# A hybrid decoder layer: products without use on TensorE in the gaps of the first transposes and of the router, and another order of the token blocks

## The chip, the cores and the metric

The kernel runs on one core of one Trainium2 chip. A core has TensorE (PE; its weight loads are listed as PEld), VectorE (DVE), ScalarE (ACT), GpSimd (POOL) and SyncE (SP), which here mostly starts transfers, and 16 DMA engines. [...] The metric is the device time of one execution, in microseconds, as the median of several runs.

## What is computed

A decoder layer for 512 tokens of width 1024 with 16 learned tokens in front: a normed input goes through one large projection into two mixers, attention and a state-space scan, whose outputs are gated, merged and added to the input; then each token goes through the best two of eight experts of its best group of four. Cut to what matters here:

```python
h = jnp.concatenate([meta, x], axis=1)               # 16 + 512 tokens
u = rmsnorm(h, norm_mix)
proj = u @ w_in                                      # 1024 -> cq, ckv, kr, z, xbc, dt, g_attn, g_ssm
merged = (sigmoid(g_attn) * (mla_branch(...) @ w_branch_attn)
          + sigmoid(g_ssm) * (ssd_branch(...) @ w_branch_ssm))
h = h + merged @ w_out
v = rmsnorm(h, norm_ffn)
g_idx = argmax(v @ w_group + b_group)                # coarse: one of 4 groups
top_vals, top_idx = top_k((v @ w_expert + b_expert)[group g_idx], 2)   # fine: 2 of 8
out = sum over experts e of comb[:, e] * ((silu(v @ w_gate[e]) * (v @ w_up[e])) @ w_down[e])
result = rmsnorm(h + out, norm_final)[:, 16:]
```

## The kernel before

The layer is written as one function with the Tile framework. Most of its instructions are put in order by a scheduler that works with its own estimate of times; where order matters, a block `with in_order(...)` fixes the order of the named engines to that of the code.

**Start.** The 528 tokens lie in five blocks: 0 to 3 of 128 and block 4 of 16. For each, `u_rstd` (L182) makes the root mean square, with ScalarE's squares `junk` and GpSimd's power. `u_turn` (L203) multiplies by that and by the gain vector `gmix` and turns the block on TensorE, four 128x128 transposes into a PSUM tile `pt` per half. Where `u_gain` (L195) has already multiplied the gain on GpSimd, ScalarE does the rest of the scaling, else VectorE does both in one instruction. `u_split` (L215) copies the turned half twice, as a rounded part `uh` on ScalarE and the rest `ul` on VectorE. Weights are split in the same way (`win0h`, `win0l`). A product of the projection is then three products, high by high, high by low and low by high. `first_mm(j, i)` (L318) makes that for weight tile j and the half i of the tokens: `first0a` and `first1a` for the first 256 tokens, `first0b` and `first1b` for the other 272. The block from L324 sets the order of all five engines' queues there.

**Middle.** Projection, scan, attention, merging and the output product keep TensorE busy from there to about 560 us.

**Router.** Around the output product's last pieces (`pout`), the rows of `h` are turned (`pvT`), multiplied with the router's weights (`plg`), and per block of tokens VectorE finds the group and the two experts (`choose`). `rank` (L1285) counts with products `rk` how many earlier tokens chose the same expert, `find_slots` and `place` (L1316) put each token's number and weight at its place in tiles `tb` and `tw` through small products, and VectorE makes of `tb` the list `idx`. Here TensorE, VectorE, ScalarE and GpSimd run in the order of the code.

**Experts.** Tokens of two experts at a time are gathered from DRAM by GpSimd (`gather`, into `xg`), 16 pairs in all. For each pair TensorE turns them (`pxT`), multiplies with the gate and up weights (`gu`, 2 MB for each expert, in two halves) and the down weights (`dn`, 1 MB), and adds the results up per token (`pc`). Seven places for `gu` and seven for `dn` are filled by transfers that SyncE starts in the order of its queue; a place is filled again when TensorE has read it. Expert 4's `gu` is loaded behind a small write, `fence` (L1429), of 128 values of four bytes each, that waits for a flag which GpSimd sets behind the first three gathers. A branch (L1446) around a part for overfull experts, that isn't taken here, stands between the router and the experts in every engine's queue.

Of the kernel before, what the change touches and what calls it, by code (L numbers as in the profile page):

```python
# [11 lines left out]
BF16 = mybir.dt.bfloat16  # L12
# [61 lines left out]
def hybrid_layer(ctx: ExitStack, tc, A, out):  # L74
# [34 lines left out]
    def ps(name):  # L109
        return psp.tile([128, 512], F32, tag="ps", name=name)  # L110
# [4 lines left out]
    def btile(name, dt=F32, n=L, tag="u"):  # L115
        t = big.tile([128, KD * L], dt, tag=tag, name=name, bufs=2 if tag == "u" else 1)
        return t[:, :KD * n].rearrange("p (k n) -> p k n", k=KD)
# [24 lines left out]
    one1 = cp.tile([1, 4], F32, name="one1")  # L142
    dve.memset(one1, 1.0)
    act.activation(one1[0:1, 0:1], one1[0:1, 0:1], AF.Square)
    xin = btile("xin", n=T, tag="v").rearrange("p k n -> p (k n)").rearrange("p (b n) -> p b n", b=4)
    xt = [[xin[:, i, hh * 512:(hh + 1) * 512] for hh in range(2)] for i in range(4)] + [glist("xm", 2, n=T, p=gq)]
    gmix = glist("gmix", 2, n=T, p=gq)
# [15 lines left out]
    load_x(1)  # L163
    load_x(2)
    ic = cs("ic")
    trib, onesb = cp.tile([128, 128], BF16, name="trib"), cp.tile([128, 128], BF16, name="onesb")
    identb, maskb = cp.tile([128, 128], BF16, name="identb"), cp.tile([128, 128], BF16, name="maskb")

    def rstd_small(dst, ssum, n, p=128, w=1):
# [25 lines left out]
    def u_gain(i, hh):  # L195
        p = 128 if i < 4 else NM
        xx = xt[i][hh][:p]
        pool.tensor_tensor(xx, xx, gmix[hh][:p], op=ALU.mult)
        gained.add((i, hh))
# [46 lines left out]
    chunk, wins = [None], {}  # L246
# [66 lines left out]
        return r  # L313


    first = [[ps(f"first{j}{x}")[:, :n] for x, n in zip("ab", (256, 272))] for j in range(2)]

    def first_mm(j, i):  # L318
        (wh, wl), (n0, n1) = wins[j], HALF[i]
# [2 lines left out]
                pe.matmul(first[j][i], x[:, k], y[:, k, n0:n1], start=(n == 0 and k == 0), stop=(n == 2 and k == KD - 1))  # L322

    with in_order(act, dve, pool, pe, nc.sync):  # L324
        u_rstd(0)
        u_turn(0, 0)
        u_rstd(1)
        u_turn(0, 1)
        u_gain(1, 1)
        u_turn(1, 0)  # L330
        u_rstd(2)
        u_gain(2, 0)
        u_gain(2, 1)
        u_turn(1, 1)
        u_split(0, 0)
        u_split(0, 1)
        u_split(1, 0)
        u_split(1, 1)
        wins[0] = proj_w(0)
        load_x(4)  # L340
        load_x(3)
        first_mm(0, 0)
        u_rstd(4)
        u_rstd(3)
        u_gain(3, 0)
        u_gain(3, 1)
        u_turn(2, 0)
        u_turn(2, 1)
        wins[1] = proj_w(1)
        first_mm(1, 0)  # L350
        nc.sync.dma_start(pv, A["pv"])
        nc.sync.dma_start(cst[:, 128:], A["cst"][:, 128:])
        nc.sync.dma_start(alog, bcast_row(A["alog"], H))

        u_turn(4, 0)
        u_turn(4, 1)
        u_split(2, 0)
        u_split(2, 1)
        u_turn(3, 0)
        u_turn(3, 1)  # L360
        u_split(4, 0)
        u_split(4, 1)
        u_split(3, 0)
        u_split(3, 1)
    for j in range(2):
        first_mm(j, 1)
    for d_, s_ in ((trib, cs("before")), (onesb, ones), (identb, ident), (maskb, mask_s)):
# [976 lines left out]
    with in_order(pe):  # L1344
        turn(0, 0)
        turn(1, 0)
        po0 = out_half(0, lambda: logits(0, 0), lambda: logits(1, 0), lambda: turn(2, 0))
        po1 = out_half(1, lambda: (logits(2, 0), turn(0, 1, po0)), lambda: turn(3, 0), lambda: (logits(0, 1), norm_v(0)))
        glx.close()
        mws["d"] = ctx.enter_context(tc.tile_pool(name="mwd", bufs=1, reuse_waits="tile", side="right"))  # L1350
        load_gu(5)
        for i in range(3, ND):
            if DN_AT[i] == "d":
                load_dn(i)
        po2 = out_half(2, lambda: (logits(3, 0), turn(1, 1, po1)), lambda: None, lambda: (logits(1, 1), norm_v(1)))
        c0, c2, c3 = choose(0, 2), choose(2, 3), choose(3, 4)
        steps(c0, 4)
        po3 = out_half(3, lambda: turn(2, 1, po2), lambda: (norm_v(2), steps(c0)), lambda: (logits(2, 1), rank(0)))
        in_turn = ctx.enter_context(ExitStack())
        in_turn.enter_context(in_order(act, dve, pool))  # L1360
        steps(c2, 5)
        find_slots(0)
        copies = turn(3, 1, po3)
        steps(c2, 3)
        copies()
        norm_v(3)
        weigh_exp(0)
        steps(c2)
        logits(3, 1)
        rank(2)  # L1370
        weigh(0)
        place(0, tb, 2)
        weigh_exp(2)
        steps(c3, 10)
        steps(c3)
        find_slots(2)
        rank(3)
        place(2, tb, 2)
        cnt = ps("cnt")
        for b in range(4):  # L1380
            pe.matmul(cnt[:, :32], onesb, oh12s[b][:, :32], start=(b == 0), stop=(b == 3))
        place(0, tw, 3)
        find_slots(3)
        weigh_exp(3)
        place(3, tb, 2)
        ovf, ovi = sm.tile([128, 1], F32, tag="sq1", name="ovf", bufs=4), cp.tile([128, 1], I32, name="ovi")
        dve.tensor_reduce(ovf, cnt[:, :32], axis=AX.X, op=ALU.max)
        dve.tensor_scalar(ovi, ovf, CAP + 0.5, None, op0=ALU.is_gt)
        weigh(2)
        lpos = cp.tile([128, 16], F32, name="lpos")  # L1390
        wsl, rsl = cp.tile([128, 16], F32, name="wsl"), cp.tile([128, 16], F32, name="rsl")
        idx = cp.tile([128, 16], I32, name="idx")
        dve.tensor_scalar(idx, tb[:, :16], float(NONE), None, op0=ALU.add)
        weigh(3)
        place(2, tw, 3)
        place(3, tw, 3)
        act.activation(lpos, tw[:, 16:32], AF.Copy)
        act.activation(wsl, tw[:, :16], AF.Copy, scale=2.0)
        in_turn.close()
# [234 lines left out]
                                 op0=ALU.mult, op1=ALU.mult)  # L1634
        dve.tensor_mul(gtab[:, :, 1], goh, ic[:, 105:109, None].to_broadcast([128, 4, 4]))

    pg = ps("pg")[:, :16].rearrange("p (b v g) -> p b v g", b=2, v=2)

    def group_places():
        for h in range(2):  # L1640
# [47 lines left out]
    LC = [slice(0, 512), slice(512, 1024)]  # L1688

    with in_order(act, dve, pe, pool, nc.sync):  # L1690
        for hh in range(2):
            turn_x(0, hh)
        group_tables()
        for p in range(16):
            end = p and p % 4 == 0
            expert_gu(p)
            for h in range(2):
                for e in (2 * p, 2 * p + 1):
                    if e != EV:
                        load_gu(e + NR + (e < EV), (h,))  # L1700
            if p < 15:
                turn_x(p + 1, 0)
                turn_x(p + 1, 1)
                if p:
                    combine(p - 1, 0, (0,))
                expert_h(p)
                if p == 0:
                    group_places()
                else:
                    combine(p - 1, 0, (1,))  # L1710
                    combine(p - 1, 1)
                y_start(p)
                y_rest(p)
                for hh in range(2):
                    for f in range(2):
                        y_mm(p, f, hh)
                    y_split(p, hh)
                    if end:
                        for b in range(2):
                            squares(b, hh)  # L1720
            else:
                y_start(p)
                y_rest(p)
                combine(p - 1, 0)
                expert_h(p, (0,))
                combine(p - 1, 1, (0,))
                y_mm(p, 0, 0)
                expert_h(p, (1,))
                y_mm(p, 0, 1)
                y_mm(p, 1, 0)  # L1730
                y_split(p, 0)
                y_mm(p, 1, 1)
                y_split(p, 1)
                combine(p - 1, 1, (1,))
            for e in range(max(2 * p + 6, ND), min(2 * p + 8, 30)):
                load_dn(e)
            if p == 12:
                for c in LC:
                    load_dn(30, [c])
                    load_dn(31, [c])  # L1740
            if p == 0:
                group_lists()
            if p == 2:
                load_gain()
            if end:
                for b in range(2):
                    norm(b)
                for b in range(2):
                    for hh in range(2):
                        scale(b, hh)  # L1750
                    store(p // 4 - 1, b)
        junk = ev.tile([128, KD, 128], F32, tag="xT", name="junk", bufs=1).rearrange("p k n -> p (k n)")
        for b in range(2):
            combine(15, 0, (b,))
            squares(b, 0, junk[:, :512])
            gained(b, 0)
        for b in range(2):
            combine(15, 1, (b,))
        squares(0, 1, junk[:, :512])
        squares(1, 1, junk[:, 512:])  # L1760
        norm(0)
        norm(1)
        for b in range(2):
            scale_gained(b, 0)
            scale(b, 1)
            store(3, b)
# [117 lines left out]
```

## Time and profile before

| | us |
|---|---|
| median of 3 runs | 820.62 |
| lowest and highest | 819.89, 820.73 |
| the profiled execution | 818.55 |
| its span, first to last instruction | 816.8 |
| TensorE busy in the span | 773.5 (95%) |
| VectorE, ScalarE, GpSimd busy | 453.8, 299.6, 141.3 |

The profile is of one execution. Times in it are counted from its first instruction. Matmuls are pipelined and their ends are modelled, so neighbours overlap a little. One product of float32 operands shows as two records of a pass each, so a row can count twice as many products as the program has. A wait in brackets at a row's end is the idle time of that engine just before it, with what ended it.

### The profile page before, as it was taken

What the parts mean: (1) busy time and instruction counts of PE and PEld (TensorE: products, weight loads), DVE (VectorE), ACT (ScalarE), POOL (GpSimd) and SP (SyncE); (2) the same over time, 40 slices, a digit from 0 to 9 for tenths busy, and PEclk for the clock granted to TensorE, in tenths of its full rate; (3) what the DMA queues carried; (4) which work ended last, traced back from release to release, by engine and by line L of the source; (5) the groups of instructions that cost most, each with busy time, mean ns of one, the idle gap of its engine ahead of it and who ended that gap; (6) DMA issues with size and microseconds to landing.
All of it is one profiled execution on the core that took longest, in us unless ns stands there. A gap on an engine that the chain in (4) does not pass through costs nothing.

```text
span 816.8 us, 11335 instructions
## 1 busy us (share of the span) xinstructions
PE 773.5 (95%) x4202; PEld 530.7 (65%) x4202; DVE 453.8 (56%) x1013; ACT 299.6 (37%) x566; POOL 141.3 (17%) x197
## 2 busy tenths in 40 slices
PE   4999999999999999999999899997799999999995
PEld 3999987677778878876665678886334343434342
DVE  3697528975366445486776766516334444543523
ACT  6554425333224473164654232422112322322313
POOL 5100002334111100005353400004100110200201
PEclk9999999999999999999999999997799999999998
DMA  7312216343222215020212395587899999999990
GB/s 256 110 58 101 104 60 203 100 129 117 91 73 95 103 41 187 29 62 9 66 41 79 92 413 200 199 311 269 210 423 418 420 418 419 419 421 419 420 383 37
DMA packets 40366, 163.39 MB, mean 200 GB/s; under 512 B 9152, under 2 KB 13648, under 8 KB 24176
## 3 DMA queue, kind: packets, MB, share of 16 engines
q1 hardware_dynamic: 35360, 154.45, 50.1%
q0 software_dynamic: 3984, 7.94, 3.0%
q8 instruction: 35, 0.57, 0.3%
q10 hardware_dynamic: 960, 0.20, 0.1%
q14 instruction: 27, 0.22, 0.1%
HBM read 159.30 MB, written 6.36 MB: 203 GB/s over the span
## 4 chain that ended last, share of the span: by engine, by line
PE 78%; DMA 8%; DVE 6%; issue 4%; ACT 2%; POOL 1%; POOLq 0%; SPq 0%; DVEq 0%; ACTq 0%
PE gu L1546 9%; DMA gu<-in_moe_gu_dram 5%; PE y L1585 5%; PE pbr L669 3%; PE pbr L672 3%; PE pbr L670 3%; PE po L872 2%; PE pc L1612 2%; PE ga L242 2%; PE gs L242 2%; PE ga L244 2%; PE ga L243 2%; PE gs L243 2%; PE pout L1094 2%; PE gs L244 2%
## 5 line engine op out<-in xcount | busy, mean ns | idle before, releaser
L1546 PE MATMUL gu<-gu,xT 128*64 128x512 f32 (+1 forms) x544 | 116.4, 572 | 2.3 <-DMA gu<-in_moe_gu_dram 2.3
L1546 PEld LDWEIGHTS gu<-gu,xT 128*64 128x64 f32 x544 | 40.0, 138 | 76.0 <-issue 63.0
L1585 PE MATMUL y<-dn,hT 128*64 128x512 f32 x256 | 58.7, 599 | 0.3 <-ACT hT L1562 0.3
L1419 POOL DMA_INDIRECT xg<-vd,idx x16 | 16.2, 1011 | 166.8 <-DVE yl L1598 106.3
L1550 DVE SCALAR_TENSOR_TENSOR hp<-th,gu 128x256 f32<-128x256 f32 (+1 forms) x17 | 6.9, 404 | 66.8 <-ACT th L1549 66.8
L818 DVE CUSTOM_DVE_ANT_0 sp<-sp,amask 128x144 f32<-128x144 f32 (+4 forms) x80 | 33.9, 459 | 18.0 <-PE sp L810 15.9
L1549 ACT ACTIVATE th<-gu,rsl 128x256 f32<-128x256 f32 (+1 forms) x17 | 7.8, 461 | 90.7 <-PE gu L1546 90.7
L1596 ACT ACTIVATE yh<-xg 128x512 fp32r<-128x512 f32 x30 | 18.9, 630 | 57.7 <-DVE xg L1595 57.7
L1595 DVE SCALAR_TENSOR_TENSOR xg<-y,wsl,xg 128x512 f32<-128x512 f32 (+1 forms) x34 | 24.2, 716 | 27.4 <-PE y L1585 27.4
L1585 PEld LDWEIGHTS y<-dn,hT 128*64 128x64 f32 x256 | 16.9, 137 | 32.8 <-issue 31.6
L1598 DVE TENSOR_TENSOR yl<-xg,yh 128x512 fp32r<-128x512 f32 x30 | 20.8, 693 | 20.9 <-ACT yh L1596 20.9
L848 PE MATMUL st<-qs,kq 97*128 97x512 f32 (+4 forms) x80 | 28.7, 359 | 1.0 <-DVE kq L793 1.0
L1612 PE MATMUL pc<-yh,st 128*128 128x512 f32 x60 | 26.3, 439 | 0.0
L1522 PEld LDWEIGHTS pxT<-cst,xg 128*128 128x128 f32 x128 | 14.4, 146 | 16.1 <-issue 12.2
L849 PE MATMUL st<-qs,kq 97*128 97x512 f32 (+4 forms) x80 | 23.7, 296 | 0.2 <-DMA qs<-rs 0.2
L857 ACT ACTIVATE pw<-st 128x512 f32<-128x512 f32 (+1 forms) x32 | 16.7, 546 | 19.7 <-PE st L853 16.1
L1524 DVE TENSOR_TENSOR xT<-pxT,pv 128x512 f32<-128x512 f32 x32 | 20.6, 682 | 5.8 <-PE pxT L1522 5.8
L1612 PE MATMUL pc<-yl,st 128*128 128x512 f32 x60 | 23.7, 396 | 0.0
L302 POOL TENSOR_TENSOR rfs<-rfm,mhalf 128x4 f32<-128x4 f32 (+1 forms) x5 | 7.6, 1521 | 92.6 <-DVE rfm L301 92.6
L878 POOL TENSOR_TENSOR pw<-pw 128x400 f32<-128x400 f32 x14 | 15.9, 1156 | 44.4 <-PE po L872 44.4
L388 DVE SCALAR_TENSOR_TENSOR cacc<-xp,cwh,cacc 128x528 f32<-128x528 f32 x30 | 22.9, 762 | 0.4
L850 PE MATMUL st<-qs,kq 97*128 97x512 f32 (+4 forms) x80 | 23.0, 294 | 0.0
(924 smaller groups left out, 2108.4 us busy)
## 6 DMA issues: line engine op xcount, KB each, us to landing
gu<-in_moe_gu_dram SPq DMA_DIRECT2D x64, 1024.0 KB, 20.5
dn<-in_moe_dn_dram SPq DMA_DIRECT2D x30, 1024.0 KB, 20.5
win<-in_win_dram SPq DMA_DIRECT2D x19, 1024.0 KB, 4.7
lm<-acd SPq DMA_DIRECT2D x16, 256.0 KB, 3.6
wbs<-in_wbs_dram SPq DMA_DIRECT2D x4, 1024.0 KB, 4.7
wba<-in_wba_dram SPq DMA_DIRECT2D x4, 1024.0 KB, 11.3
wo<-in_wout_dram SPq DMA_DIRECT2D x4, 1024.0 KB
ce<-acd SPq DMA_DIRECT2D x16, 128.0 KB, 7.4
```

What stands on the lines that cost most here:

```text
L242: pe.matmul(dst, ah, bh, start=(i == 0), stop=False)
L243: pe.matmul(dst, ah, bl, start=False, stop=False)
L244: pe.matmul(dst, al, bh, start=False, stop=(i == n - 1))
L669: pe.matmul(pb_, wh[:, k], oh[k], start=(k == 0), stop=False)
L670: pe.matmul(pb_, wh[:, k], ol[k], start=False, stop=False)
L672: pe.matmul(pb_, wl[:, k], oh[k], start=False, stop=(k == last))
L818: dve.tensor_tensor_reduce(s_, s_, amask[:, L - nk + n0:L - nk + n1], 1.0, -3.0e38, op0=ALU.add, op1=ALU.max, accum_out=mx[:, n_:n_ + 1])
L848: pe.matmul(d_, kh_[0:97, kb], qh_[0:97, q0:q1], start=True, stop=False)
L1546: pe.matmul(gu[f][r, :2 * n], xT[p][:, k, r], w, start=(k == 0), stop=(k == KD - 1), skip_group_check=True)
L1585: pe.matmul(yp[hh][e * 64:(e + 1) * 64], hT_[p][:, f, e * 64:(e + 1) * 64], dns[(2 * p + e) % ND][:, f, hh * 512:(hh + 1) * 512], start=(f ...
L1595: dve.scalar_tensor_tensor(y, yp[hh][:, c.start - hh * 512:c.stop - hh * 512], wsl[:, p:p + 1], y, op0=ALU.mult, op1=ALU.add)
L1612: pe.matmul(sums[b, hh], st[:, b * 128:(b + 1) * 128], x[:, c], start=(n == 0 and p % 4 == 0), stop=(n == 1 and p % 4 == 3), skip_group_ch ...
```

## The change

A helper `keep_busy(dst, n)` issues n products of a 128x128 tile `trib`, that is zero at the start, with one of its columns broadcast to 512; their result in `dst` is not used. (Later `trib` holds a triangle of ones, whose first column is zero too.) 18 of them stand at the head of TensorE's work, then 2, 3 and 6 between the first transposes, 3, 2, 10, 2 and 6 among the router's products and 3 ahead of the experts' first transposes. They write into PSUM tiles that are in use later anyway. Beside that, the second weight tile is split and multiplied (`proj_w(1)`, `first_mm(1, 0)`) before blocks 2 and 3 are turned, block 3 is turned ahead of block 4, and its gain goes to VectorE (no `u_gain(3, ..)`).

```diff
+    trib = cp.tile([128, 128], BF16, name="trib")
+    dve.memset(trib, 0.0)
+
+    def keep_busy(dst, n):
+
+        for _ in range(n):
+            pe.matmul(dst, trib, trib[:, 0:1].to_broadcast([128, 512]), start=True, stop=True, skip_group_check=True)
...
+        keep = banks[1][1]
+        keep_busy(keep, 18)
         u_rstd(0)
         u_turn(0, 0)
+        keep_busy(keep, 2)
         u_rstd(1)
         u_turn(0, 1)
+        keep_busy(keep, 3)
         u_gain(1, 1)
         u_turn(1, 0)
...
         u_turn(1, 1)
+        keep_busy(keep, 6)
...
+        wins[1] = proj_w(1)
         first_mm(0, 0)
         u_rstd(4)
         u_rstd(3)
-        u_gain(3, 0)
-        u_gain(3, 1)
+        first_mm(1, 0)
         u_turn(2, 0)
         u_turn(2, 1)
-        wins[1] = proj_w(1)
-        first_mm(1, 0)
+        u_turn(3, 0)
+        u_turn(3, 1)
+        u_split(2, 0)
...
         find_slots(0)
+        keep_busy(tw, 3)
         copies = turn(3, 1, po3)
+        keep_busy(tw, 2)
         steps(c2, 3)
...
         place(0, tb, 2)
+        keep_busy(tw, 10)
         weigh_exp(2)
...
         rank(3)
+        keep_busy(tw, 2)
         place(2, tb, 2)
...
         place(3, tw, 3)
+        keep_busy(tb, 6)
         act.activation(lpos, tw[:, 16:32], AF.Copy)
...
     with in_order(act, dve, pe, pool, nc.sync):
+        keep_busy(pgb, 3)
         for hh in range(2):
             turn_x(0, hh)
```

What stands in a row on TensorE at the start, before:

```order
L213 MATMUL pt<-cst,xin 128x128 x16
L322 MATMUL first0a<-uh,win0h 128x256 x8
L322 MATMUL first0a<-ul,win0h 128x256 x8
L322 MATMUL first0a<-uh,win0l 128x256 x8
L213 MATMUL pt<-cst,xin 128x128 x8
L322 MATMUL first1a<-uh,win1h 128x256 x8
L322 MATMUL first1a<-ul,win1h 128x256 x8
L322 MATMUL first1a<-uh,win1l 128x256 x8
L213 MATMUL pt<-cst,xm_96 128x16 x4
L213 MATMUL pt<-cst,xm_97 128x16 x4
L213 MATMUL pt<-cst,xin 128x128 x8
```

And now, from the last filler of the group of six on (`xm` is block 4, `xin` the others):

```order
L151 MATMUL first1b<-trib 128x512
L331 MATMUL first0a<-uh,win0h 128x256 x8
L331 MATMUL first0a<-ul,win0h 128x256 x8
L331 MATMUL first0a<-uh,win0l 128x256 x8
L331 MATMUL first1a<-uh,win1h 128x256 x8
L331 MATMUL first1a<-ul,win1h 128x256 x8
L331 MATMUL first1a<-uh,win1l 128x256 x8
L221 MATMUL pt<-cst,xin 128x128 x16
L221 MATMUL pt<-cst,xm_98 128x16 x4
L221 MATMUL pt<-cst,xm_99 128x16 x4
```

The transposes of blocks 2 and 3 have moved behind `first1a`, and block 3 ahead of block 4.

On ScalarE at the same place, before:

```order
L235 ACTIVATE win0h<-win_169 128x1024
L189 ACTIVATE junk,ssq<-xm_96 16x512
L189 ACTIVATE junk,ssq<-xm_97 16x512
L186 ACTIVATE junk,ssq<-xin 128x1024
L208 ACTIVATE xin<-xin,rst 128x512 x2
L235 ACTIVATE win1h<-win_169 128x1024
L175 ACTIVATE uh<-pt 128x4x128 x2
L208 ACTIVATE xin<-xin,rst 128x512 x2
L385 ACTIVATE xp<-first1a 128x256
```

And now:

```order
L243 ACTIVATE win0h<-win_199 128x1024
L243 ACTIVATE win1h<-win_199 128x1024
L197 ACTIVATE junk,ssq<-xm_98 16x512
L197 ACTIVATE junk,ssq<-xm_99 16x512
L194 ACTIVATE junk,ssq<-xin 128x1024
L216 ACTIVATE xin<-xin,rst 128x512 x2
L397 ACTIVATE xp<-first1a 128x256
L183 ACTIVATE uh<-pt 128x4x128 x4
```

The split of the second weight tile has moved to the front, and the first copy of a result, `xp`, ahead of the `uh` of blocks 2 and 3.

On SyncE behind the branch, before (`gu_5319` is expert 4's place):

```order
L1446 UNCONDITIONAL_BRANCH x2
L1048 DMA dn_5803<-in_moe_dn_dram 128x2048
L1048 DMA dn_5805<-in_moe_dn_dram 128x2048
L1429 DMA fence<-flag 128x1
L1039 DMA gu_5319<-in_moe_gu_dram 128x2048 x2
```

And now, ahead of the branch:

```order
L1462 TENSOR_LOAD ovi
L1462 ISA x2
L1446 DMA fence<-flag 128x1
L1051 DMA gu_5370<-in_moe_gu_dram 128x2048
L1463 COMPARE_AND_BRANCH
```

The code there is the same in both; the scheduler has put `fence` and the first half of expert 4's load ahead of the branch, and the second half and the two `dn` loads are left behind it.

## Rows read from the trace of the kernel before

**Rows 1.** The chain that ended last, first 31 us: start us, us, what.

```profile
12.63 1.96 PE pt L213 x8
...
16.21 5.10 PE first0a L322 x24
21.30 0.87 PE pt L213 x8
22.18 2.81 PE first1a L322 x24
...
26.86 0.77 PE first0b L322 x4
```

**Rows 2.** Instructions in order of time, first 30 us: start us, us, engine, line, operation.

```profile
9.04 1.12 PE L213 MATMUL pt<-cst,xin 128*128 128x128 f32 x4 [9.04 <-DVE rs L171]
...
12.67 1.69 ACT L175 ACTIVATE uh<-pt 128x512 fp32r<-128x512 f32 x3
...
13.28 2.66 DVE L176 TENSOR_TENSOR ul<-pt,uh 128x512 fp32r<-128x512 f32 x4 [0.66 <-ACT uh L175]
14.61 0.60 ACT L175 ACTIVATE uh<-pt 128x512 fp32r<-128x512 f32 x1 [0.26 <-PE pt L213]
15.10 1.05 ACT L235 ACTIVATE win0h<-win 128x1024 fp32r<-128x1024 f32 x1
...
20.76 2.19 DVE L236 TENSOR_TENSOR win1l<-win,win1h 128x1024 fp32r<-128x1024 f32 x1 [2.02 <-ACT win1h L235]
...
22.87 1.40 DVE L210 SCALAR_TENSOR_TENSOR xm<-xm,rst,gmix 16x512 f32<-16x512 f32 x2
...
25.03 0.38 ACT L385 ACTIVATE xp<-first1a 128x256 f32<-128x256 f32 x1 [0.94 <-PE first1a L322]
```

**Rows 3.** Stretches: us, busy of five engines, granted clock, DMA share, GB/s.

```profile
562.00:563.40 1.40, 1.01 (x10) 1.02 (x10) 1.29 (x7) 0.19 (x2) 1.06 (x4) 1.00 0.82 246
563.40:580.50 17.10, 9.23 (x90) 6.80 (x90) 8.36 (x47) 4.15 (x12) 7.45 (x22) 0.50 0.78 276
```

**Rows 4.** TensorE's instructions in order of time, 557 to 574 us.

```profile
557.97 0.98 PE L1186 MATMUL plg<-wrt,vbT 128*128 128x40 f32 x8
...
562.39 1.08 PE L1186 MATMUL plg<-wrt,vbT 128*128 128x40 f32 x8 [0.52 <-DVE vbT L1168]
...
563.55 1.04 PE L1328 MATMUL tb<-ru 128*64 128x16 f32 x16
567.51 0.25 PE L1292 MATMUL rk<-ohc,onesb 128*128 128x36 bf16 x3 [2.91 <-DVE ru L1308]
...
568.33 0.83 PE L1328 MATMUL tb<-ru 128*64 128x16 f32 x8 [0.53 <-POOL ru L1313]
```

**Rows 5.** The chain that ended last, 560 to 595 us.

```profile
570.37 0.42 PE tb L1328 x8
...
571.72 4.61 DMA xg<-vd,idx
```

**Rows 6.** SyncE's queue, 575 to 577.3 us.

```profile
576.22 0.97 SPq L1048 DMA_DIRECT2D dn<-in_moe_dn_dram  x2
577.23 2.37 SPq L1429 DMA_DIRECT2D fence<-flag  x1
```

**Rows 7.** Stretches of the expert stage, columns as in rows 3.

```profile
592.00:792.00 200.00, 196.79 (x944) 81.85 (x942) 85.83 (x178) 51.83 (x96) 22.41 (x25) 1.00 1.01 419
578.00:584.00 6.00, 6.00 (x24) 1.90 (x25) 3.52 (x18) 0.00 (x0) 0.00 (x0) 0.79 0.99 389
584.00:592.00 8.00, 7.17 (x46) 3.01 (x44) 3.24 (x8) 2.11 (x4) 0.00 (x0) 1.00 0.99 130
```

**Rows 8.** The page's groups: busy us, mean ns, idle before and its cause.

```profile
L1546 PE MATMUL gu<-gu,xT 128*64 128x512 f32 (+1 forms) x544 | 116.4, 572 | 2.3 <-DMA gu<-in_moe_gu_dram 2.3
```

**Rows 9.** TensorE's instructions in order of time, 560 to 640 us.

```profile
578.34 8.12 PE L1546 MATMUL gu<-gu,xT 128*64 128x512 f32 x32
...
592.42 7.04 PE L1546 MATMUL gu<-gu,xT 128*64 128x512 f32 x32
```

More of the change, by code (lines that the diff above doesn't have):

```diff
@@ L165, in hybrid_layer @@
     ic = cs("ic")
-    trib, onesb = cp.tile([128, 128], BF16, name="trib"), cp.tile([128, 128], BF16, name="onesb")
+    onesb = cp.tile([128, 128], BF16, name="onesb")
     identb, maskb = cp.tile([128, 128], BF16, name="identb"), cp.tile([128, 128], BF16, name="maskb")
@@ L313, in rms_feat @@
         return r
-    first = [[ps(f"first{j}{x}")[:, :n] for x, n in zip("ab", (256, 272))] for j in range(2)]
+    banks = [[ps(f"first{j}{x}") for x in "ab"] for j in range(2)]
+    first = [[b[:, :n] for b, n in zip(bb, (256, 272))] for bb in banks]
     def first_mm(j, i):
@@ L353, in hybrid_layer @@
         nc.sync.dma_start(alog, bcast_row(A["alog"], H))
+        u_split(2, 1)
         u_turn(4, 0)
         u_turn(4, 1)
[L357 to L360, printed above, removed]
+        u_split(3, 0)
+        u_split(3, 1)
         u_split(4, 0)
         u_split(4, 1)
-        u_split(3, 0)
-        u_split(3, 1)
     for j in range(2):
@@ L1635, in group_tables @@
         dve.tensor_mul(gtab[:, :, 1], goh, ic[:, 105:109, None].to_broadcast([128, 4, 4]))
-    pg = ps("pg")[:, :16].rearrange("p (b v g) -> p b v g", b=2, v=2)
+    pgb = ps("pg")
+    pg = pgb[:, :16].rearrange("p (b v g) -> p b v g", b=2, v=2)
     def group_places():
```

## The prediction

> **What bounds the kernel now.** I read four views in this order. First the chain of work that ended last, in the first 31 us [rows 1]: it goes through the transposes `pt` and the two half products `first0a` and `first1a`, and from 26.86 us on, where `first0b` starts, TensorE has hardly a gap for a long time. A shift of that moment is a shift of all that follows up to the router. What the reader should see is that the same work has two prices: 24 products of 256 columns take 5.10 us in `first0a` and 2.81 us in `first1a`, and eight transposes take 1.96 us before and 0.87 us after. [...] The column of the granted clock says 1.00 in both, since no change of level is on record before; here only the durations tell.
>
> Second, the stretches around the router [rows 3]: the granted clock falls to 0.50 at 563.4 us, after TensorE had stood still twice and run small products, and stays there to 580.5 us, some 4 us after the experts' first tokens had landed. Third, the router's own rows [rows 4, 5]: up to 567.5 us VectorE, ScalarE and GpSimd carry the chain; from 568.33 to 570.79 us it runs on TensorE's small placing products, then over VectorE's list `idx` to GpSimd's gathers, whose first lands at 576.3 us.
>
> Fourth, the expert stage. TensorE is busy for 196.79 of the 200 us from 592 on, and yet the transfers set the end: the DMA engines are full at 419 GB/s over the same 200 us [rows 7], and where TensorE stands still ahead of the products `gu` it waits for their weights, 2.3 us in all [rows 8]. A stage that lives on transfers ends at the time at which they start plus a fixed amount of bytes, whatever TensorE does ahead of it. So of the router and of the first pair of experts only that counts which lets the weights start earlier.
>
> **The change part by part.** A filler is a 512-column product: by `first0a`, 5.10/24 x 2 = 0.425 us at the lower level, by `first1a` 0.234 us at the upper.
>
> *Start.* 18 fillers begin at about 1 us; before, TensorE's first work was at 9.04 us [rows 2]. All at the lower level they are over at 1 + 18 x 0.425 = 8.65 us, ahead of the first `pt`, so they cost nothing. In the router's neighbourhood the clock came back after some 4 us of work; so it should be up at about 5 us here, and the groups of 2, 3 and 6 behind it are to keep it up. At the upper level the eight transposes end at 12.63 + 0.87 = 13.5 us, and ScalarE's fourth `uh`, which waited for them until 14.61, follows its three others at 12.67 + 1.69 = 14.36 [rows 2]. `win0h` (1.05 us) is then done at 15.9, and `first0a` starts at 15.95 in place of 16.21, also because VectorE's four `ul` end at 15.94 anyway. The six fillers (1.4 us at the upper level, 2.55 at the lower) lie in this gap.
>
> *Order of blocks.* `first1a` now follows `first0a` at once: 48 products at 2.81/24 = 0.117 us end at 21.6 us, instead of 24.99. `win0l` and `win1l` are ready for that: VectorE's `win1l` took 2.19 us while GpSimd multiplied block 3 by the gain [rows 2]; that work of GpSimd has gone to VectorE as two `xin`, like the two `xm` some 0.7 us each, and `win1l` should be faster without it. But what had stood between the two products now stands behind: `xp` of `first1a` (0.38 us), which comes ahead of block 2's `uh` in ScalarE's queue, one `uh` (0.60), two `ul` (2.66/4 each), the two `xm` (1.40), the transposes and the copy of the 16 leftover tokens (some 0.7): 4.4 us, so `first0b` starts at 26.0 to 26.2 in place of 26.86. I take **0.7 us earlier**. Only part of the 2.3 us that `first0a` saves comes out, since VectorE and ScalarE are late next. Bounds: 1.2 us earlier if the copies overlap more than that; 2.6 us later if the level does not rise (the six fillers then hold `first0a` back to 14.6 + 2.55 = 17.15 us, it ends at 22.25, `first1a` at 25.05, and with the 4.4 us behind it `first0b` starts at 29.45).
>
> *Router.* Fillers of 3 and 2 lie in gaps of some half a microsecond (0.52 ahead of `plg`) and fill them at the upper level; a tenth of a microsecond of delay there is within the bounds. The group of 10 stands between the placing products that end at 563.55 + 1.04 = 564.59 and `rk` at 567.51 [rows 4], a gap of 2.91 us: 2.34 us at the upper level, which fits, but 4.25 us at the lower, which would put `rk` at 568.84, 1.33 us late, with VectorE, ScalarE and the list `idx` behind it. The next two stand in a gap of 0.53 us: 0.47 fits, 0.85 costs 0.32. What a held clock gives: only the 2.46 us from 568.33 to 570.79 are TensorE's on the chain. No row has these products at the upper level; the nearest are eight `plg` products, 0.98 us at the upper level and 1.08 with the fall inside [rows 4], a tenth, and the transposes' halving at the far end. So 0 to 1.2 us, and I take **0.2 us earlier**, nearest to `plg`, whose columns are few too; the other end is 1.65 us later. [...]
>
> The six fillers behind the placing products and the three ahead of `pxT` may delay the first `pxT` (1.28 us at the lower level); the level that they hold up saves 8.12 - 7.04 = 1.08 us in the first `gu` [rows 9]. Both are TensorE's time in a stage that lives on transfers: I count 0.
>
> *SyncE's queue.* The scheduler has also moved the small write `fence` and one half of a `gu` load ahead of SyncE's branch; the two `dn` loads, that started at 576.22 [rows 6], now come behind it. `fence` waits for GpSimd's flag behind the three gathers, so the branch is taken only then and the rest of the loads follow some 3 us later than that. But the rows show that the 2 MB of `dn` did not buy that much: after the 128 four-byte pieces of `fence`, which were queued behind `dn`, the rate falls from 389 to 130 GB/s for 8 us [rows 7]. With `fence` first, the slow stretch comes first, with one `gu` half to move in it, and the full rate comes that much earlier. By 592 us before has moved 6 x 0.389 + 8 x 0.130 = 3.4 MB; with the slow stretch from 577.5 to 585.5 and full rate behind it: 1.0 + 6.5 x 0.42 = 3.7 MB, 0.8 us better; with 2.4 us lost behind the branch 2.7 MB, 1.6 us worse. I take **0**, bounds 1.5 us earlier and 2 us later.
>
> Sum against the profiled execution (818.55 us, its span and 1.8 us around it): 818.55 - 0.7 - 0.2 = 817.65. The median of the runs before lies 2.07 us above that execution, so I forecast 820.62 - 0.9 = **819.7 us**.
>
> **Rivals.** (a) *The slow stretch shrinks.* `fence` runs on nearly idle engines, and its writes don't hold up full queues: up to 8 x (1 - 130/419) = 5.5 us of transfers come back, of which TensorE can surely use what it lost waiting for `gu`, 2.3 us. For it: the drop comes right with the small pieces. Against: the pieces themselves may be what is slow. With 2.3 us: 817.4. [...]
> (b) *TensorE binds the expert stage after all*, and the 1.08 us of `gu` come through: 818.6. For it: 196.79 us busy of 200. Against: the full DMA engines beside it [rows 7] and the waits [rows 8].
> (c) *The fillers are in the way in the router.* The level falls among the small products anyhow, and `rk` and the placing come 1.65 us late: 819.9 + 1.65 = 821.6. It decides once the ten are not through at 567.5 us, so when the level is low before some 566 us.
> (d) *The change doesn't do what it says:* a product of zeros, with one column broadcast, doesn't raise the clock. Then the start costs 2.6 us and the router 1.65: 820.62 + 4.25 = 824.9. It decides if the level isn't up by 16 us.
> (e) *The loads behind SyncE's branch start late* and the slow stretch stays: 819.7 + 2 = 821.7.
>
> **How the numbers follow.** Forecast 0.47; (a) 0.14; (b) 0.13; (c) 0.10; (d) 0.08; (e) 0.08. A measurement of this kernel can tell about 0.2%, 1.64 us, from no change: faster is below 818.98, slower above 822.26. Faster: (a), (b) and the lower edge of the forecast, 0.32. Slower: (d) and (c) with (e) together, 0.14. Within: 0.54. The range, 816.8 to 822.4, takes in the forecast with its own bounds, (b), (c), (e) and most of (a), and leaves out (d) and that part of (a) in which TensorE can use more than its waits.
>
> **What would show it.** At the start: `first0a` in about 2.8 us from 16.0, `first0b` at 26.1; if `first0a` takes 5 us, (d). In the router: a granted clock of 1.00 at 566 us and `rk` behind VectorE, not behind fillers; a 0.50 there with `rk` late is (c). The gathers should land some 0.9 us earlier. Then the GB/s after `fence`: a stretch at 130 that begins at about 577 is my forecast, no such stretch is (a), an empty one of 2 us is (e). If TensorE's waits for `gu` at the end are gone and the time still fell, (b). The forecast is wrong if TensorE's long gapless run starts later than at 26.9 us, or if the weights reach 419 GB/s more than 2 us off 591 us.

## The result: 0.6% slower, and why the transfers came late

The changed kernel takes 824.3 us (median of 6 runs, 821.7 to 827.1) against 819.75 us for the kernel before (6 runs, 819.1 to 820.7): a ratio of 1.0059, 95% interval 1.0044 to 1.0073. The forecast was 819.7 us, no change, within 816.8 to 822.4. The profiled execution of the changed kernel has a span of 822.8 us, 6.0 us more than the one before.

The start did what was forecast. TensorE's instructions of the changed kernel in order of time (start us, us, engine, line, operation; idle time before it and its cause):

```profile
1.06 5.91 PE L151 MATMUL first1b<-trib 128*128 128x512 bf16 x18 [1.06 <-DVE trib L146]
...
15.81 1.21 PE L331 MATMUL first0a<-uh,win0h 128*128 128x256 f32 x8 [0.70 <-ACT win0h L243]
...
21.60 1.91 PE L221 MATMUL pt<-cst,xin 128*128 128x128 f32 x16
24.95 0.39 PE L221 MATMUL pt<-cst,xm 16*128 16x16 f32 x4 [1.44 <-DVE xm L218]
...
25.93 0.77 PE L331 MATMUL first0b<-uh,win0h 128*128 128x272 f32 x4
```

The granted clock stands at 1.00 or 0.50 in the records of both traces; these two are called the upper and the lower level here. The first record, of 1.00, begins at 4.80 us; in the kernel before it begins at 20.68 us, inside `first0a`. The fillers start 0.427 us apart ahead of 4.80 us and 0.218 behind it (0.425 and 0.234 were forecast). The eighteen ended at 6.97 us, `first0a` ran at the upper level (2.95 us from its start to that of `first1a`), and `first0b` started 0.93 us earlier than in [rows 1]. The same 0.93 us is there at every product up to 144 us. Then it is lost. TensorE waits 1.69 us for VectorE there, in both kernels, and in this execution the granted clock falls to 0.50 behind the wait, from 144.75 to 148.16 us. Two stretches of the changed kernel around it (us, busy of five engines, granted clock, DMA share, GB/s):

```profile
26.00:144.00 118.00, 116.97 (x793) 106.28 (x793) 79.53 (x140) 52.62 (x88) 10.98 (x10) 1.00 0.31 103
144.00:149.00 5.00, 4.33 (x12) 3.47 (x13) 4.84 (x9) 0.00 (x0) 4.58 (x5) 0.66 0.00 1
```

Behind it the changed kernel is 0.62 us late instead of 0.93 early: 1.55 us. Some 0.8 us more went between 430 and 474 us (one of the small loads there, `li`, starts 3.2 us behind the `lid` that it waits for, 1.4 us in the kernel before; why stays open), and the router began 1.4 us late. In the router the fillers were not in the way: `rk` waited for VectorE (1.05 us), not for them, the level held to 571.4 us in place of 563.4 [rows 3], and 0.1 us came back. The row of `rk`:

```profile
568.91 0.23 PE L1304 MATMUL rk<-ohc,onesb 128*128 128x36 bf16 x3 [1.05 <-DVE ru L1320]
```

The rest, 4.6 of 6.0 us, came behind the router. SyncE's queue in the changed kernel, to be read beside [rows 6]:

```profile
576.98 0.34 SPq L1446 DMA_DIRECT2D fence<-flag  x1
577.53 13.78 SPq L1051 DMA_DIRECT2D gu<-in_moe_gu_dram  x2
591.63 1.56 SPq L1060 DMA_DIRECT2D dn<-in_moe_dn_dram  x2
593.24 2.14 SPq L1051 DMA_DIRECT2D gu<-in_moe_gu_dram  x4
```

The 13.78 us span two halves of one load: the first is issued ahead of the branch, the second only behind it. The waits of SyncE's queue say what lay between (who waits, for whom, us in all, times, the longest):

```profile
SPq L1463 <- SPq L1463: 12.5, 2, 11.0
```

L1463 is the branch; SyncE itself is named as the cause, so nothing of the program held it. The branch stood at 577.9 us, the first instruction behind it at 589.0. In the kernel before the same place took 2.6 us, at 570.7 us, with nothing of `fence` under way. The stretches of the changed kernel:

```profile
578.00:586.00 8.00, 8.00 (x35) 3.68 (x34) 3.94 (x18) 0.00 (x0) 0.00 (x0) 0.77 1.05 61
586.00:592.00 6.00, 5.17 (x38) 2.31 (x34) 2.49 (x7) 1.90 (x3) 0.00 (x0) 1.00 0.37 132
592.00:792.00 200.00, 195.45 (x920) 82.03 (x916) 84.11 (x175) 50.85 (x94) 22.41 (x25) 1.00 1.01 418
```

Read the last two columns together. From 578 to 586 us the DMA engines are full (1.05) and move 61 GB/s: few pieces that each take long. The long ones are the load's own: in the trace's records of single pieces those of 8 KB take up to 8.1 us there, against 0.31 us in the median from 600 to 780 us, while the four-byte ones of this queue stand with 9 ns each. So where this text says slow pieces, they are the loads', slowed by the small writes beside them (b_fence_one and b_fence_apart show it, below). From 586 to 592 us they have little to do (0.37): the pieces of 8 KB are fast again (0.31 us in the median, 1.2 the longest), and from 589 to 592 us the share is 0.14. Before, in the same 16 us from 576 to 592, 234 GB/s were moved, now 103: 2.1 MB less, 5 us at the full rate. The rate is as full as ever later on [rows 7], only it starts with more to do, and TensorE pays at the end. The `gu` group of the page, for [rows 8], with 4.3 us of waits in place of 2.3:

```profile
L1563 PE MATMUL gu<-gu,xT 128*64 128x512 f32 (+1 forms) x544 | 118.3, 571 | 4.3 <-DMA gu<-in_moe_gu_dram 4.3
```

And the last `gu` that waits, from TensorE's instructions in order of time (it starts at 794.79 us in the kernel before, 6.0 us earlier):

```profile
800.80 3.67 PE L1563 MATMUL gu<-gu,xT 128*64 128x256 f32 x30 [1.10 <-DMA gu<-in_moe_gu_dram]
```

### The profile page after: what moved, and what is told of

Its sections match the earlier page's. It is cut to its first block, busy times and chain, and to the rows that moved or that the text cites. A ratio compares the mean times of both kernels' runs of the same rounds, so it can differ in the third digit from the quotient of the medians.

```text
span 822.8 us, 11445 instructions
## 1 busy us (share of the span) xinstructions
PE 787.7 (96%) x4257; PEld 534.6 (65%) x4257; DVE 455.8 (55%) x1016; ACT 298.3 (36%) x564; POOL 138.7 (17%) x195
## 5 line engine op out<-in xcount | busy, mean ns | idle before, releaser
L1563 PE MATMUL gu<-gu,xT 128*64 128x512 f32 (+1 forms) x544 | 118.3, 571 | 4.3 <-DMA gu<-in_moe_gu_dram 4.3
L1563 PEld LDWEIGHTS gu<-gu,xT 128*64 128x64 f32 x544 | 42.1, 138 | 77.8 <-issue 59.2
L1629 PE MATMUL pc<-yh,st 128*128 128x512 f32 x60 | 26.2, 437 | 0.0
```

Source lines behind the costliest of these rows:

```text
L1563: pe.matmul(gu[f][r, :2 * n], xT[p][:, k, r], w, start=(k == 0), stop=(k == KD - 1), skip_group_check=True)
L1629: pe.matmul(sums[b, hh], st[:, b * 128:(b + 1) * 128], x[:, c], start=(n == 0 and p % 4 == 0), stop=(n == 1 and p % 4 == 3), skip_group_ch ...
```

## The experiments

Three questions: is it SyncE's queue; what makes the slow stretch; and where does the gain of the start go. All ratios are to the kernel before, run beside on the same chip.

| kernel | what it is | us | ratio, 95% interval |
|---|---|---|---|
| changed | all of the change | 824.3 | 1.0059, 1.0044 to 1.0073 |
| a_fence_late | changed, `fence` behind the `dn` loads | 820.6 | 1.0017, 1.0005 to 1.0030 |
| b_tail | before, with the last nine fillers | 823.6 | 1.0059, 1.0044 to 1.0073 |
| b_fence_one | before, `fence` of 1 value | 815.5 | 0.9958, 0.9945 to 0.9970 |
| b_fence_apart | before, `fence`'s values apart | 814.2 | 0.9953, 0.9936 to 0.9971 |
| a_fence_one | changed, `fence` of 1 value | 819.1 | 0.9991, 0.9974 to 1.0008 |
| a_start_only | start of the change alone | 820.5 | 1.0019, 1.0002 to 1.0037 |
| b_fill_only | start's fillers, old order | 818.5 | 0.9991, 0.9976 to 1.0006 |
| a_order_only | new order, no fillers | 821.8 | 1.0032, 1.0011 to 1.0052 |
| a_no_tail_one | changed, no last nine, 1 value | 815.7 | 0.9967, 0.9952 to 0.9982 |
| a_gap | the same, one gap filled | 815.2 | 0.9960, 0.9944 to 0.9976 |
| a_full | the same, three gaps filled | 813.3 | 0.9924, 0.9901 to 0.9947 |
| b_best | old order, two gaps filled | 813.4 | 0.9926, 0.9909 to 0.9942 |

### SyncE's queue

**a_fence_late**: all of the change, but the order of SyncE's queue as it was.

```diff
-    with tc.issue_after(nc.sync.dma_start(fence, flag).ins):
-        load_gu(EV)
...
     for i in range(3, ND):
         if DN_AT[i] == "e":
             load_dn(i)
+    with tc.issue_after(last_dn[0].ins):
+        fenced = nc.sync.dma_start(fence, flag).ins
+    with tc.issue_after(fenced):
+        load_gu(EV)
```

> The changed kernel with all its fillers, but the write fence and both halves of the gu load behind it are held behind the two dn loads, as in the kernel before. Theory Q (the queue): SyncE takes its branch only behind fence, the code behind the branch and the loads then come 13 us late (11.0 us of wait in the changed kernel), and that is some 4.6 of the 6.0 us of span that were lost. Then dn starts at about 577.5 us, and the time is 824.3 - 4.6 = 819.7 us, between 818.7 and 820.7. Theory T (the fillers behind the placing products and ahead of pxT hold TensorE up, and that lasts to the end): nothing comes back, 823.5 to 824.5. Theory M (the loss arises ahead of the router, by the lower clock level at 144.7 us and a late small load at 462 us, and the rest is chance): 823 to 824.5.

820.6 us: 3.4 us of the 4.8 came back (0.42% of 819.5), with every filler in place. SyncE's wait behind the branch is short again (waits of SyncE's queue):

```profile
SPq L1463 <- SPq L1463: 2.8, 1, 2.8
```

So theories T and M fall as the main cause. The 0.17% that is left lies ahead of the queue, as far as this trace tells: `dn` starts at 579.56 us in it, 3.3 us later than in [rows 6], behind falls of the clock level at 26, 146 and 473 us.

**b_tail**: the reverse, the kernel before with nothing but the last two groups of fillers.

```diff
+        keep_busy(tb, 6)
         act.activation(lpos, tw[:, 16:32], AF.Copy)
...
     with in_order(act, dve, pe, pool, nc.sync):
+        keep_busy(pgb, 3)
         for hh in range(2):
             turn_x(0, hh)
```

> The kernel before with nothing added but the last two groups of fillers (six behind the placing products, three ahead of pxT); the scheduler then puts fence ahead of SyncE's branch, as in the changed kernel. Theory Q: the loss of the changed kernel without its start, 819.75 + 4.6 = 824.3 us, between 823 and 825.5, with SyncE's wait behind the branch over 8 us. Theory T: pxT comes 0.8 us later as in the changed kernel, 820.6 us at the most if that lasts, with fence's place of no account. Theory M: 819.8 us, no change.

The loss of the whole change, 1.0059, from nine products without use. Six of them stand ahead of TensorE's branch, and the scheduler, which goes by its own times for them, now puts `fence` ahead of SyncE's; which of the two groups does it was not tried. SyncE's queue and waits in this kernel (its branch is L1455):

```profile
576.25 0.34 SPq L1438 DMA_DIRECT2D fence<-flag  x1
576.81 0.88 SPq L1047 DMA_DIRECT2D gu<-in_moe_gu_dram  x2
592.43 0.95 SPq L1056 DMA_DIRECT2D dn<-in_moe_dn_dram  x2
```

```profile
SPq L1455 <- SPq L1455: 13.8, 2, 11.8
```

Theory Q stands from both sides: `fence` put back behind the loads heals, `fence` moved ahead of the branch without the rest of the change hurts as much as all of it.

### What makes the slow stretch

**b_fence_one** and **a_fence_one**: the same edit on the kernel before and on the changed one. It leaves out 127 of the 128 values, which nobody reads.

```diff
-    with tc.issue_after(nc.sync.dma_start(fence, flag).ins):
+    with tc.issue_after(nc.sync.dma_start(fence[0:1], flag[0:1]).ins):
```

> The kernel before, but fence writes 1 value instead of 128 (it waits for the same flag). Theory F (the 128 four-byte pieces of fence hold the 8 KB pieces of the weights up for some 8 us): the stretch at 130 GB/s from 584 to 592 us is gone, the weights run at over 380 GB/s from 578 us on, and the time falls by the 2.3 us that TensorE waits for gu, up to the 5.5 us of transfers that come back: 814.3 to 817.5 us. Rival G (the gathers' rows, the loads of code behind the branches or the loads themselves make the slow stretch): it stays, 819.5 to 820 us.

> The changed kernel, but fence writes 1 value instead of 128; it still stands ahead of SyncE's branch. Theory Q with F: the code behind the branch is loaded without the stretch of slow pieces, SyncE's wait behind the branch falls from 11.0 to about 3 us, the dn and gu loads start at about 581 us in place of 591, and 4.6 us and 2.3 to 5.5 us more come back: 814.2 to 817.4 us. Q without F (the code's load waits behind the half load of gu, or always takes that long behind a late branch): SyncE's wait stays over 8 us, 823 to 824.5 us. T or M: 823.5 to 824.5 us.

In the kernel before the slow stretch of [rows 7] is gone (stretch of b_fence_one), and with it all of TensorE's waits for `gu` (the page's group):

```profile
580.00:592.00 12.00, 11.17 (x57) 4.30 (x57) 6.15 (x25) 1.78 (x3) 0.00 (x0) 0.89 1.00 410
```

```profile
L1546 PE MATMUL gu<-gu,xT 128*64 128x512 f32 (+1 forms) x544 | 113.8, 572 | 0.0
```

0.42% faster, 3.4 us, within the 2.3 to 5.5 that were expected: theory F. In the changed kernel one value brings 0.7%, but only back to the level of before: 819.1 us, not the 814.2 to 817.4 that Q with F had said. SyncE's waits of a_fence_one, and two stretches of it:

```profile
SPq L1463 <- SPq L1463: 6.5, 2, 5.0
```

```profile
578.00:582.00 4.00, 3.60 (x20) 1.80 (x21) 2.77 (x14) 0.00 (x0) 0.00 (x0) 1.00 0.81 263
582.00:586.00 4.00, 4.00 (x22) 1.42 (x20) 1.07 (x6) 0.00 (x0) 0.00 (x0) 1.00 0.18 51
```

Without slow pieces the wait is 5.0 us, not the 3 that were expected, and the DMA engines still run nearly empty from 582 to 586 us. SyncE's first instruction behind the branch comes at 582.9 us, a second wait takes 1.5 us, and the second half of `gu` is issued at 584.9 us. So of the 11.0 us, 5.0 are there with one value in `fence` too, with transfers under way, and 6.0 come only with the slow pieces.

**b_fence_apart**: 128 values again, each 4096 bytes from the next.

```diff
-    fence = drp.tile([128, 1], F32, name="fence")
+    fence = drp.tile([128, 1024], F32, name="fence")
...
-    nc.sync.dma_start(fence, flag)
+    nc.sync.dma_start(fence[:, 0:1], flag)
```

> The kernel before, with fence still writing 128 values of 4 bytes, but each to a place 4096 bytes from the next, and not side by side within 512 bytes. If the number of four-byte pieces holds the weights up: the slow stretch stays, 819.5 us. If it is that the pieces go to the same few lines of memory: the stretch at 130 GB/s is gone or is under 2 us, 815 to 817 us.

814.2 us, a little under what was expected and as fast as one value (stretch of b_fence_apart):

```profile
580.00:592.00 12.00, 11.16 (x64) 4.28 (x62) 4.55 (x15) 2.53 (x4) 0.00 (x0) 0.99 1.01 416
```

It is not the number of pieces, nor their four bytes: it is 128 pieces side by side in 512 bytes of memory. (The wider tile can also lie elsewhere in memory as a whole; that was not varied by itself.) Both kernels write 128 pieces of four bytes, and only the one with its pieces side by side holds the weights up (130 GB/s from 584 to 592 us [rows 7], against 416 here). Why neighbours hurt is not shown.

### Where the start's gain goes

**a_start_only**, **b_fill_only** and **a_order_only** take the start apart; none has fillers in the router, and `fence` stands where it stood.

The changed kernel to a_start_only:

```diff
-        keep_busy(tw, 3)
         copies = turn(3, 1, po3)
-        keep_busy(tw, 2)
...
-        keep_busy(tw, 10)
...
-        keep_busy(tw, 2)
...
-        keep_busy(tb, 6)
...
-        keep_busy(pgb, 3)
```

> The start of the change alone: the fillers of 18, 2, 3 and 6 and the other order of the blocks, none of the router's fillers; fence stands behind the dn loads as in the kernel before and writes 128 values. If the start's 0.93 us come through and the lower clock level at 145 us falls in some executions of any kernel: 819.5 - 0.9 = 818.6 us. If that fall belongs to the start (a TensorE that runs 0.93 us earlier meets it, at 1.55 us a time): 819.5 + 0.6 = 820.1 us or more, and the trace has 0.50 at about 145 us.

a_order_only is a_start_only without its four groups `keep_busy(keep, ...)`; b_fill_only is the kernel before with these four:

```diff
+        keep_busy(keep, 18)
         u_rstd(0)
         u_turn(0, 0)
+        keep_busy(keep, 2)
...
         u_turn(0, 1)
+        keep_busy(keep, 3)
...
         u_turn(1, 1)
+        keep_busy(keep, 6)
```

> The kernel before with the start's fillers alone (18, 2, 3 and 6): the blocks in their old order, no fillers in the router. Theory O (the start's gain is eaten by falls of the clock level, and one of these places is made by the new order, which leaves TensorE only 16 transposes between first1a at 21.6 us and first0b at 25.6): without the new order there is no fall at 25 us; first0a takes 2.8 us, and the time is that of before or up to 0.9 us under it, 818.0 to 819.0 us beside a before of 818.9. Theory P (any earlier and longer high level brings more falls later on, at 145 and 459 us): 819.5 to 820.5 us, and the trace has a fall at 145 or 459 us.

> The other order of the blocks alone, no fillers anywhere. first0a takes 5.1 us at the lower level again, first1a follows at once, and the level rises in it. Theory O: the new order puts TensorE's idle stretch behind first1a, and the level falls at about 25 us in part of the executions (1.4 us each): 819 to 820.5 us beside a before of 818.9. If the order does nothing by itself: 818.5 to 819.2 us, and no fall at 25 us.

The start alone is 0.19% slower, which is what a_fence_late had left of the loss. That is the time of its second theory, but its trace has the falls at 25 and 459 us, not at 145. With the old order the fillers are worth more than with the new one: `first0b` starts at 24.88 us, 1.98 earlier than before. The new order alone makes it 0.69 us later (27.55 us), and a_order_only is the slowest of the three, 0.32% or 2.6 us, more than theory O had said. (These are single traces: with the start as before, `first0b` starts at 26.31 to 26.86 us in four of them, with the whole start of the change at 25.33 to 25.93 us in six.) Together they give 25.58 us, and a price beside it: between `first1a` and `first0b` TensorE has only transposes and 1.4 us of idle time, and in a_start_only the level falls behind that. Three stretches of a_start_only:

```profile
21.60:25.30 3.70, 1.99 (x21) 1.71 (x19) 2.87 (x5) 2.44 (x6) 0.00 (x0) 1.00 0.19 70
25.30:28.70 3.40, 3.40 (x18) 3.36 (x18) 1.83 (x9) 0.22 (x1) 0.00 (x0) 0.50 0.00 0
...
458.80:462.20 3.40, 3.40 (x6) 1.51 (x7) 1.97 (x4) 1.58 (x2) 1.15 (x1) 0.50 0.01 2
```

The first fall costs 1.41 us: `first0b` was 1.28 us early, the first `xbc9a` behind it is 0.13 us late. Over all traces: at 25 to 27 us the level falls in 3 of the 6 kernels with the start's fillers, the new order and no filler in that place, and in none with the old order. At 145 us it falls in 7 of 11 traces, that of b_fence_one among them, which has no filler at all; between 457 and 474 us in 6 of 12. a_order_only has none at 25 us, but the level low from 145.6 to 152.4 us, behind which it is 3.5 us late. So theory O is right in that the new order costs (b_fill_only gave the time it forecast, P's it missed), and wrong in that the place at 25 us were all of it. P's sign is in the trace of b_fill_only all the same: the level falls at 144.4 and at 458.5 us, and of the 1.98 us that TensorE is early, 0.45 are left behind the first fall. Whether a TensorE that comes at another moment meets the later falls more often than the kernel before stays open.

**a_no_tail_one, a_gap, a_full**: the changed kernel without the last nine fillers and with one value; then with fillers where TensorE stands still at the places of the falls.

```diff
+                for _ in range(7 if (c, g) == (1, 1) else 0):
+                    pe.matmul(pcb[:, 128:], trib, trib[:, 0:1].to_broadcast([128, 384]), start=True, stop=True, skip_group_check=True)
                 dve.tensor_mul(cbm[:, g], pcb[:, :128], tri)
```

And a_full beyond a_gap:

```diff
+        keep_busy(keep, 6)
         u_turn(4, 0)
...
         pl = ps("pl")
+        keep_busy(pl, fill)
...
-        pl7 = row_sums(PP[7])
+        pl7 = row_sums(PP[7], 6)
```

> The changed kernel without its last two groups of fillers (six and three), so that fence goes behind the dn loads, and with fence writing 1 value. If queue, pieces of fence and start add up: 819.5 - 4.0 (measured for one value) - 0.9 - 0.1 = 814.5 us. If the fillers of the start and of the router's middle cost something of their own, it lies above the 815.5 us of the kernel before with one value.

> As a_no_tail_one, with seven fillers of 384 columns more in the gap of 1.7 us at 143 to 145 us, in which TensorE waits for VectorE's bd. If the lower clock level behind this gap comes from the standing still, it is gone at 145 us in the trace, and the 1.5 us that it takes in executions that have it come back: up to 1.5 us below a_no_tail_one, 813.0 to 814.5 us. If the fillers are in the way (pcb and VectorE's cbm come later): up to 1 us above it. If the fall is of another cause, the trace still has 0.50 there and the time is the same.

> As a_gap (start, new order, the router's middle fillers, one value in fence, fillers in the gap at 143 to 145 us), with six fillers more in each of the two other places after which the level falls: the gap of 1.4 us ahead of the last transposes (23.4 to 24.9 us) and the 1.9 us ahead of the last pl (457.3 to 459.2 us). If the falls come from standing still: none at 25, 145 or 459 us, and the falls that a_no_tail_one had in part of its executions come back, 813.0 to 814.5 us, with a narrower spread than its 5.3 us. If the fillers are in the way: 815.5 us or more.

a_no_tail_one missed the 814.5 us of the sum and is no better than the kernel before with one value: the start costs what it brings, as in a_start_only. TensorE in the filled gap of a_gap, where it idles 0.44 us in place of 1.69:

```profile
142.55 1.32 PE L589 MATMUL pcb<-trib 128*128 128x384 bf16 x7
144.31 0.48 PE L250 MATMUL z<-uh,win19h 128*128 128x512 f32 x1 [0.44 <-DVE bd L618]
```

No trace with this gap filled has a fall at 145 us (3 of 3); with 7 falls in 11 traces without it, that would come by chance about once in twenty. By itself it moved the time by less than can be told (815.2 us, not the 813.0 to 814.5 expected), and the level still fell at 457 us in a_gap. With all three filled (stretch of a_full) the level holds from 26 us to the router:

```profile
26.00:565.00 539.00, 532.58 (x2988) 419.94 (x2989) 335.66 (x739) 217.54 (x410) 94.92 (x121) 1.00 0.35 120
```

a_full is 0.76% faster than the kernel before, and its six runs lie within 2.0 us (812.6 to 814.6), where a_no_tail_one's twelve spread over 5.3. Its level falls once ahead of that stretch, from 10.7 to 14.1 us, between the start's fillers. The trace of the kernel before has no fall from 26 us to the router either: what the filled gaps bring is shown by the ratio and the spread, and that they bring it through the level is argued from them.

**b_best**: a_full with the blocks in their old order, and without the six fillers ahead of the last transposes.

```diff
-        wins[1] = proj_w(1)
         first_mm(0, 0)
...
-        first_mm(1, 0)
         u_turn(2, 0)
         u_turn(2, 1)
...
+        wins[1] = proj_w(1)
+        first_mm(1, 0)
```

> All that helped, together: the start's fillers with the blocks in their old order, the router's middle fillers (3, 2, 10 and 2, none of the last two groups), fence with 1 value behind the dn loads, seven fillers in the gap at 143 to 145 us and six ahead of the last pl. If the old order is the better one by what first0b showed (24.88 us with fillers and the old order, 25.6 to 26.5 us with fillers and the new one): 0.7 to 1.6 us under a_full, 811.7 to 812.6 us at its level of 813.3 us, a ratio of 0.990 to 0.992. If the two orders are worth the same once the gaps are filled: a ratio of 0.992 to 0.993.

`first0b` starts at 25.09 us in its trace, 1.43 us earlier than in a_full's with its fall at 10.7 us, and the span is 810.8 us against 812.1; but the medians of the two are the same, so a preference for the old order is not shown here.

## Right and wrong, step by step

**The bound** was read rightly: the end is set by when the weights start. **The start** up to `first0b` was right (26.0 to 26.2 said, 25.93 measured; level up at "about 5 us", 4.8 measured). Wrong was to let its 0.7 us run on to the end: "TensorE has hardly a gap for a long time" skips the gap of 1.69 us at 144 us, which takes up to 1.55 us. The sum also took the fillers and the new order as one step; they are two, of opposite sign (1.98 us earlier, 0.69 later): the VectorE and ScalarE that are "late next" are so in the new order.

**The router's** 0.2 us was right (0.1). The placing products follow the clock: sixteen records of `tw` took 0.66 us at the upper level, 1.07 at the lower in the kernel before (first the changed kernel, then the one before):

```profile
570.57 0.66 PE L1340 MATMUL tw<-cst,ru 128*64 128x32 f32 x16
569.30 1.07 PE L1328 MATMUL tw<-cst,ru 128*64 128x32 f32 x16
```

**SyncE's queue is the step that failed**: taken at 0, bounds 1.5 us earlier to 2 later, measured 3.4 (a_fence_late) to 4.8 us later (b_tail). The sum had the mechanism, that the branch is taken only behind `fence`, and rival (e) was it, with 2 us as its price. (e)'s sign came, too: the engines are nearly empty from 589 to 592 us, and 410 GB/s are reached only at 594. The term in it was mis-sized: "the rest of the loads follow some 3 us later" was the 2.6 us that SyncE needs behind its branch in the kernel before. Here it was 11.0. And the full rate behind the slow stretch, which the sum set against it, did not come, as the engines had little to do (0.37 from 586 to 592 us).

A DMA queue that the profile calls instruction moved one block of 8 KB between 587.3 and 589 us:

```profile
q14 instruction: 1, 0.01, 1.1%
```

In the trace's records this block ends at 587.7 us, 1.3 us ahead of the first instruction behind the branch. In each of the fourteen traces one such block ends 1.1 to 1.5 us ahead of that instruction. What differs is how long behind the branch it ends: 1.5 us in the kernel before, 3.9 in a_fence_one, 9.8 in the changed kernel, 10.6 in b_tail. So it looks as if SyncE waits for this block, and as if the block comes late when the loads are slow. That it is code, and SyncE's, is my reading of the queue's name and of these times; the profile names no owner.

**The rivals.** (a) had the mechanism too: the small pieces do hold full queues up, and without them 3.4 us come back; but to move them to the front does not free anything, because SyncE then goes on behind its branch only after 11.0 us, in place of 2.6. What (a) held against itself, that the small pieces may be what is slow, is not so: the loads' pieces are (up to 8.1 us, the small ones 9 ns each). (b): TensorE does bind the experts, as soon as the slow stretch is gone (no wait for `gu` in b_fence_one). (c) and (d) fell: the level held to 571.4 us, and with products of zeros it was up at 4.8 us. **The last two groups of fillers** were counted as 0 on TensorE, which was about right there (`pxT` 0.8 us later, 0.3 at the first pair); their effect was on the scheduler, and through it on a queue that they never touch.

## What to carry to other kernels

Ahead of a branch, look at what stands in the DMA queues at that moment: the 2.6 us read off the kernel before, where the branch came ahead of `fence` and the loads, were 11.0 us here behind them. Do not let many small writes of a marker go to neighbouring addresses while large loads run: one value did the same here, and was worth 0.4% (b_fence_one). Fillers for TensorE paid here once the gaps behind which the level had fallen were filled too (a_full, 0.76% faster), and are to be kept away from places where a scheduler may read them as work (b_tail, 0.59% slower).

## What the runs showed of the hardware

- 128 writes of four bytes side by side (512 bytes in all) went with a slow stretch of the loads: 130 GB/s from 584 to 592 us in the kernel before, 61 from 578 to 586 in the changed one, with full engines (0.99 and 1.05). From 580 to 592 us it was 410 GB/s with one write (b_fence_one) and 416 with the writes 4096 bytes apart (b_fence_apart). The loads' pieces of 8 KB took up to 8.1 us in the changed kernel's slow stretch, 0.31 us in the median from 600 to 780 us.
- SyncE's wait behind its branch was 2.5 to 3.3 us where the branch came ahead of `fence` and the loads (eleven traces; 2.6 in the kernel before), 5.0 us with a load under way (a_fence_one), and 11.0 and 11.8 us with the load slowed by such writes (changed kernel, b_tail). The first instruction behind it followed the end of a block in a queue called instruction by 1.1 to 1.5 us in every trace.
- With products of zeros, one column broadcast, from 1.06 us on, TensorE's granted clock was on record as 1.00 from 4.80 us on in the changed kernel, in place of 20.68 us.
- TensorE's granted clock fell to 0.50 behind the stop of 1.69 us at 144 us in 7 of 11 traces, in none of 3 with that gap filled. That fall cost 1.55 us in the changed kernel, the one at 25 us cost 1.41 us in a_start_only.
